# Mixture of experts on one Trainium2 core: four experts side by side in 32 slots each, their weights in 8 KB runs

## The chip, the core and the metric

The program runs on one core of a Trainium2 chip. The metric is the device time of one execution in microseconds (us), the median of several runs; lower is better. Engines are named as in the profile: PE is TensorE's matmuls and PEld its weight loads (LDWEIGHTS), DVE is VectorE, ACT ScalarE, POOL GpSimd, SP the engine that here only issues transfers (DMAs). MB is 10^6 bytes, KB 1024 bytes; "a piece" below is one 1024 KB load, 1.0486 MB.

## The reference, cut to what matters

Two transformer blocks run over 256 tokens of width 1024. The first has three attention branches; the second has a mixer, a cross attention and, last, a mixture of 32 experts. The change is in the last part, of which this is the core:

```python
xf = rmsnorm(h) * g                                  # 256 tokens x 1024
g_sel = argmax(softmax(xf @ w_group + b_group))      # one of 4 groups
top_p, top_i = top_k(softmax(logits of the 8 experts of the group), 2)
gate = p_g * top_p / sum(top_p)
...
for each expert e, for the tokens that took it:
    hid = silu(x @ w_gate[e]) * (x @ w_up[e])        # 1024 -> 512
    out = hid @ w_down[e]                            # 512 -> 1024
y[token] += gate * out;   h = h + y                  # float32 throughout
```

An expert has three float32 matrices of 2 MiB each: 6 MiB an expert, 201.3 MB for all 32. Each token takes two experts, so there are 512 assignments, 16 an expert on the average. Worked out with the reference's own router on the inputs that it draws by default, the fullest expert has 29 tokens.

## The kernel before, in words

**Up to about 600 us** the kernel works through the products with weights of both blocks (class `Stream`, line 213 issues their matmuls). Loads of weights run ahead on SP's queue, into a ring of 23 buffers of 8 KB per partition (`SLOTS = 23`, tag `s8`); the n-th piece goes into the buffer of piece n - 23 and its DMA waits until the last matmul that reads that piece is done. The experts' weights follow in the same stream and the same ring, so their first 23 pieces are fetched while the earlier products still run.

**The router** (lines 1640 to 1730) gives `rank[token, expert]`, the place of a token among those of its expert (0 where it isn't taken), and `gate`.

**The experts** are worked two at a time, in 16 pairs. An expert has `E_CAP = 64` slots; the two experts of a pair share the 128 slots, that is TensorE's 128 columns, one in columns 0 to 63 and the other in 64 to 127 (`HALVES`). For a pair:

- `select` (line 1768, on POOL except for the first pair) makes `sel[token, slot]`, the row's scale where the token has the slot, and `selg`, the gate there. It takes four TENSOR_SCALARs of 128x64 for each.
- `gather` (line 1783) is a matmul of `h` with `sel`; it gives the slots' inputs transposed, a 128x128 block for each of the 8 blocks of K, and line 1785 multiplies in the gain `gffn`.
- `up_and_gate` (line 1825): for each of the 8 blocks of K and for both experts a matmul of 64 columns by 512, for `w_gate` and then for `w_up`: 32 matmuls in the program, 64 instructions in the profile, since a float32 matmul is two instructions there. Lines 1831 to 1836 make the hidden values; `hid_T` (line 1845) transposes them.
- `down` (line 1854): 16 such matmuls, 32 instructions, over the two halves of the output's columns. `combine` (line 1865) gives the slots' outputs back to the tokens with `selg` transposed (line 1808), four matmuls of 128x512, and sums over the pairs in PSUM.

A pair has 12 pieces: two halves of each matrix for both experts. Each is loaded as `(k p) f -> p k f`: partition p gets rows p, 128 + p, 256 + p and 384 + p of the half, 2 KB of each (of `w_down`, half the columns of 512 rows, again 2 KB). The last six pieces are loaded in quarters of 1 KB runs, so that the last pair can begin on half the columns. The next pair's loads are issued as buffers come free; nothing else is on SP's queue until the output. PE's program order is fixed: up and gate of a pair, the gather of the next pair's inputs, `hid_T`, `down`, `combine`. The last pair does its four quarters of the output's columns one after the other (lines 1900 to 1925).

If an expert has more tokens than slots, a loop at the end (from line 1931) goes over all 32 experts again, loading their weights once more; with at most 29 tokens it isn't entered, before or after.

Of the kernel before, what the change touches and what calls it, by code (L numbers as in the profile page):

```python
# [15 lines left out]
OP = mybir.AluOpType  # L16
# [4 lines left out]
NT = 2          # token tiles  # L21
# [79 lines left out]
class Stream:  # L101
    """The products with weights, in one order: loads run ahead as far as there is room, the weights' split
    into two float32r parts two units ahead, and pump() issues the next units of products."""

    def __init__(self, k, parts):
        """parts: pairs of a job and a piece of its K"""
# [20 lines left out]
    def fetch(self):  # L127
# [53 lines left out]
    def idle(self):  # L181
        """no unit can be issued"""
# [5 lines left out]
    def pump(self, n=1):  # L188
        for _ in range(n):
# [11 lines left out]
            # low x high, high x high and high x low parts, the low parts of the weights last as they come last  # L201
# [31 lines left out]
class Kit:  # L233
# [42 lines left out]
    def take(self, shape, dt=F32):  # L276
        """one of the 8 KB pieces"""
# [4 lines left out]
    def rotations(self, *counts):  # L282
        """functions that hand out the 2 KB parts of one piece, counts[i] of them, in turn"""
# [15 lines left out]
    def carver(self):  # L299
        """a function that cuts tiles out of one piece"""  # L300
# [15 lines left out]
    def give(self, n):  # L316
        """n pieces have seen their last use"""
# [4 lines left out]
def block_kernel(ctx: ExitStack, tc: tile.TileContext, a: dict, out: bass.AP):  # L322
# [6 lines left out]
    # ================================================================ the products with weights, in order  # L329
# [53 lines left out]
    for e0 in range(0, 32, 2):  # L383
        pa_, pb_ = expert_srcs(e0), expert_srcs(e0 + 1)
# [40 lines left out]
    ACT.activation(sm(1), mhalf, AF.Sin)    # has the tables of the sine, which the copies need too, loaded early  # L425
# [6 lines left out]
    # later[p, k] = 1 where k > p  # L432
# [52 lines left out]
    def row_ss(src, c, ss, at=None, junk=None):  # L485
        """sums of squares of part c (a half) of the rows of src [P, NT, D], into ss [P, NT, parts]"""
# [5 lines left out]
    def row_scale(ss, name):  # L492
        """1 / rms of rows of D elements"""
# [13 lines left out]
    def split_evac(src, dstH, dstL, scale):  # L507
        """dstH + dstL = scale * src, dstH the rounded part"""
# [24 lines left out]
    def rope(x_, table, dst=None):  # L533
        """dst, x_ [P, NT, heads, 2 * half]; table: cosines and signed sines [P, NT, 2 * half], gains included"""
# [11 lines left out]
    def head_ss(src, heads, d):  # L546
        """sums of squares of the heads; src [P, heads, d]"""
# [9 lines left out]
    def out_of(dst, src, scale, on_dve):  # L557
        """dst = scale * src, from PSUM"""
# [25 lines left out]
    def pipeline(units, stages, fill):  # L584
        """stage s of unit i is issued in step i + s, products with weights after each step"""
# [16 lines left out]
    def exps(sc, rs, cols_, sums):  # L602
        """exp(rs * sc - max) of sc [P, n, nk]; column cols_[i] of rs and of sums belongs to sc[:, i]"""
# [13 lines left out]
    def weights_T(e):  # L617
        """transposes [P keys, n * blocks, P queries] of e [P, n, nk]"""
# [51 lines left out]
    def silu2(dsts, srcs, half):  # L670
        """dst = silu(2 * half * src) / half, for each token tile"""
# [6 lines left out]
    # ================================================================ first block  # L678
    # ---- x, transposed; its rows' scale comes in after the products
# [11 lines left out]
    # ---- rotary tables  # L691
# [7 lines left out]
    cs = cut([P, NT, 3, 16])       # cosines, sines, their opposites  # L699
# [22 lines left out]
    # cosines and signed sines of both halves, with the gains  # L722
# [16 lines left out]
    # masks: bf16 zeros and ones, times BIG on the tensor engine  # L739
# [10 lines left out]
    # ---- latent parts of branch B  # L750
# [15 lines left out]
    # evac of products that become heads: natural, one tile per token tile  # L766
# [1231 lines left out]
```

## Time and profile before

| | us |
|---|---|
| median of 3 runs (1085.7 to 1088.31) | 1085.85 |
| span of the profiled execution, first to last instruction | 1084.3 |
| start of the first pair's up and gate | 600.4 |
| start to start of one pair and the next | 29.96 |
| PE busy in the span | 1050.6 |

The median is 1.55 us above the profiled span; all sums below are made on the span and those 1.55 us are added at the end. The span falls into two parts: to 600 us the products of both blocks, with the experts' first loads under their last 80 us, and from there the 16 pairs. PE's busy time covers 97% of the span, but a busy PE may be one matmul after another or two side by side; which, is told by the time from one to the next.

### The profile page before, as it was taken

The page shows a single profiled execution, that of the slowest core. Times are in us where ns is not written, and L with a number is a line of the kernel's source. Part 1 is how long each engine was busy: PE and PEld are TensorE (multiplying, and loading weights), DVE is VectorE, ACT ScalarE, POOL GpSimd, SP SyncE. Part 2 cuts the span into 40 slices and gives each one's busy share as a digit, 9 for nine tenths or more (in the row PEclk, how much of TensorE's full clock was granted, in tenths as well). Part 3 has the DMA queues.
Part 4 walks back from the last instruction along what each step waited for, and adds up shares of the span by engine and source line. Part 5 has one row for each costly group of instructions (what it writes and reads, how often), then busy time and mean ns, then how long its engine had stood idle before and what let it go on. Part 6 is the DMA issues. An engine that isn't in the chain of part 4 may idle for free.

```text
span 1084.3 us, 13738 instructions
## 1 busy us (share of the span) xinstructions
PE 1050.6 (97%) x5377; PEld 690.3 (64%) x5377; DVE 463.1 (43%) x830; ACT 351.3 (32%) x669; POOL 178.9 (16%) x275
## 2 busy tenths in 40 slices
PE   8999999999999999999999999999999999999997
PEld 8978877788788877868878443444444444334444
DVE  5689675667666576767644311111111111101113
ACT  6656564454544653555543000000000000000000
POOL 4444001021131022200010211111111110111100
PEclk9999999999999999999999999999999999999999
DMA  6942434354564533635699899999999999999995
GB/s 214 385 141 83 154 117 155 117 194 146 167 169 155 192 118 115 231 119 187 237 308 331 317 387 386 386 387 386 386 387 386 386 386 386 387 386 386 386 372 176
DMA packets 153857, 289.91 MB, mean 267 GB/s; under 512 B 5841, under 2 KB 22078, under 8 KB 153790
## 3 DMA queue, kind: packets, MB, share of 16 engines
q1 hardware_dynamic: 152862, 286.46, 74.6%
q0 software_dynamic: 928, 2.54, 0.9%
q8 instruction: 44, 0.72, 0.3%
q14 instruction: 23, 0.19, 0.0%
HBM read 287.94 MB, written 1.05 MB: 267 GB/s over the span
## 4 chain that ended last, share of the span: by engine, by line
PE 88%; DVE 7%; ACT 2%; DMA 1%; issue 1%; SPq 0%; POOL 0%; ACTq 0%; POOLq 0%; DVEq 0%
PE pg L213 35%; PE psc L1825 20%; PE psc L1854 10%; PE pg L1865 5%; PE ptp L1783 3%; PE po L1783 3%; DVE s L165 2%; PE po L657 2%; DVE wk L1785 1%; PE ptp L1845 1%; PE psc L526 1%; PE psc L1165 1%; PE ptp L623 1%; PE psc L1521 1%; DVE s L560 1%
## 5 line engine op out<-in xcount | busy, mean ns | idle before, releaser
L213 PE MATMUL pg<-s,s 128*128 128x512 f32 (+5 forms) x2076 | 454.2, 376 | 4.2 <-ACT s L164 1.9
L213 PEld LDWEIGHTS pg<-s,s 128*128 128x128 f32 x2076 | 365.7, 189 | 71.3 <-ACT s L164 2.7
L1825 PE MATMUL psc<-s,wk 128*64 128x512 f32 (+1 forms) x1024 | 220.2, 587 | 0.0
L165 DVE TENSOR_TENSOR s<-s,s 128x1024 fp32r<-128x1024 f32 (+4 forms) x170 | 197.2, 1191 | 49.4 <-ACT s L164 49.2
L164 ACT ACTIVATE s<-s 128x1024 fp32r<-128x1024 f32 (+4 forms) x170 | 160.9, 995 | 13.3 <-DVE s L165 7.5
L1825 PEld LDWEIGHTS psc<-s,wk 128*64 128x64 f32 x1024 | 72.0, 137 | 136.2 <-issue 131.3
L1854 PE MATMUL psc<-s,wk 128*64 128x512 f32 (+1 forms) x544 | 113.9, 570 | 0.3 <-DMA s<-in_w_e_down_dram 0.3
L1832 DVE SCALAR_TENSOR_TENSOR wk<-wk,psc 128x512 f32<-128x512 f32 x16 | 11.0, 688 | 165.7 <-ACT wk L1831 165.7
L1854 PEld LDWEIGHTS psc<-s,wk 128*64 128x64 f32 x544 | 37.9, 137 | 64.4 <-issue 59.4
L1768 POOL TENSOR_SCALAR masks<-slot,rank,tiny 128x64 f32<-128x64 f32 x60 | 33.6, 577 | 233.9 <-PE po L1783 222.4
L477 POOL TENSOR_TENSOR sm<-sm,tiny 128x8 f32<-128x8 f32 (+2 forms) x28 | 36.0, 1297 | 179.6 <-DVE sm L481 146.4
L1865 PE MATMUL pg<-wk,wr 128*128 128x512 f32 (+1 forms) x136 | 59.8, 581 | 0.0
L1846 ACT ACTIVATE wk<-ptp 128x512 f32<-128x512 f32 (+1 forms) x17 | 9.7, 572 | 145.2 <-PE ptp L1845 145.2
L611 ACT ACTIVATE s<-psc,sm,tiny 128x256 f32<-128x256 f32 (+1 forms) x64 | 32.9, 520 | 72.1 <-DVE sm L608 71.6
L1768 POOL TENSOR_SCALAR selg<-slot,rank,el 128x64 f32<-128x64 f32 x60 | 33.6, 577 | 129.6 <-PE ptp L1808 129.6
L1858 DVE COPY wk<-psc 128x512 f32<-128x512 f32 (+1 forms) x18 | 11.7, 648 | 101.1 <-PE psc L1854 101.1
L1836 DVE TENSOR_TENSOR wk<-wk,psc 128x512 f32<-128x512 f32 (+1 forms) x16 | 10.7, 671 | 86.2 <-PE psc L1825 86.2
L1865 PEld LDWEIGHTS pg<-wk,wr 128*128 128x128 f32 x136 | 24.4, 189 | 35.1 <-issue 34.9
L1831 ACT ACTIVATE wk<-psc 128x512 f32<-128x512 f32 x16 | 9.6, 597 | 107.2 <-PE psc L1825 107.2
L1809 ACT ACTIVATE wr<-ptp 128x256 f32<-128x256 f32 x16 | 6.1, 383 | 107.3 <-PE ptp L1808 107.3
L1783 PEld LDWEIGHTS ptp<-masks,h 128*128 128x128 f32 x256 | 29.9, 191 | 14.1 <-issue 12.2
L1783 PE MATMUL ptp<-masks,h 128*128 128x128 f32 x256 | 33.2, 282 | 1.6 <-DVE masks L1768 1.0
(325 smaller groups left out, 885.8 us busy)
## 6 DMA issues: line engine op xcount, KB each, us to landing
s<-in_w_e_gate_dram SPq DMA_DIRECT2D x64, 1024.0 KB
s<-in_w_e_up_dram SPq DMA_DIRECT2D x62, 1024.0 KB
s<-in_w_e_down_dram SPq DMA_DIRECT2D x60, 1024.0 KB
s<-in_w_in_dram SPq DMA_DIRECT2D x36, 1024.0 KB
s<-in_w_ckv_dram SPq DMA_DIRECT2D x8, 1024.0 KB
s<-in_w_branch_dram SPq DMA_DIRECT2D x6, 1024.0 KB
s<-in_w_mem_kv_dram SPq DMA_DIRECT2D x4, 1024.0 KB
s<-in_w_out_dram SPq DMA_DIRECT2D x4, 1024.0 KB
```

Of the source, the lines that this page charges most:

```text
L164: self.k.nc.scalar.activation(hl[:, 0], w, AF.Copy)
L165: self.k.nc.vector.tensor_tensor(out=hl[:, 1], in0=w, in1=hl[:, 0].bitcast(F32), op=OP.subtract)
L213: mm(j.outs[t], lhsT=x_, rhs=hl[:, int(c == 2), i, :], start=step == ends[t][0], stop=step == ends[t][1])
L477: POOL.tensor_tensor(out=dst, in0=src, in1=e_.to_broadcast(shape), op=OP.pow)
L611: ACT.activation(e[:, i, :], sc[:, i, :], AF.Exp, bias=nb[:, i:i + 1], scale=rs[:, c:c + 1], accum_out=sums[:, c:c + 1])
L657: PE.matmul(o[:, hd % (out_heads or heads), :], lhsT=pt[:, i * nkt + kt, :], rhs=vals(kt, hd), start=(kt == 0), stop=(kt == nkt - 1))
L1768: eng.tensor_scalar(sel[:, t, 64 * i:64 * i + 64], slot, rank[:, t, e0 + i:e0 + i + 1], factor(t, e0 + i), op0=OP.is_equal, op1=OP.mult)
L1783: PE.matmul(tp[:, kb, :], lhsT=h[:, t, (k0 + kb) * P:(k0 + kb + 1) * P], rhs=sel[:, t], start=(t == 0), stop=(t == 1))
L1825: PE.matmul(p_[s0:s0 + sn, :], lhsT=xs[k0 // 4][:, kb, s0:s0 + sn], rhs=tiles(m, i, k0 // 4)[:, kb, cols], start=(k0 + kb == 0), stop=(k0 ...
L1854: PE.matmul(p_[s0:s0 + sn, :], lhsT=hT[:, kb, s0:s0 + sn], rhs=tiles(2, i, c)[:, kb, cols], start=(kb == 0), stop=(kb == 3))
L1858: DVE.tensor_copy(od, p_)
L1865: PE.matmul(outs[t][c], lhsT=sgT[:, t, :], rhs=od, start=start, stop=stop)
```

## The change

`E_CAP` is 32 and `QUAD` is 4: four experts at a time in 8 quads, each with 32 of the 128 columns, so 24 pieces a quad. `gate` and `up` of all quads but the first, and `down` of all quads but the last, are loaded as `(p k) f -> p (k f)`: partition p gets four neighbouring rows (two of `w_down`, whose piece is then 256 rows with all columns), 8 KB in one run. The order of the rows within K is thereby another one, so `gather_part` takes every fourth column of `h`, `hid_T` every second of `hid`, and a gain in the same order (`gpack`) is loaded. `select` makes all 128 slots with two TENSOR_TENSORs, now always on DVE. The last four pieces, not six, come in 1 KB runs.

```diff
-E_CAP = 64
+E_CAP = 32
+QUAD = 4
...
-        if i < n - 6:
+        if i < n - QUAD:
             dma(out=w, in_=src)
-        elif i % 2 == (n - 1) % 2:
+        elif i == n - 1:
             for c in range(2):
-                for x in (i - 1, i):
+                for x in range(n - QUAD, n):
                     cuts = [slice(0, 4)] if (c, x) != (1, n - 1) else [slice(0, 2), slice(2, 4)]
...
+    def packed_srcs(e):
+        r = []
+        for name in ("w_e_gate_2", "w_e_up_2", "w_e_down_2"):
+            src = a[name][0, e]
+            n, per = src.shape[0] // 2, src.shape[0] // 256
+            r.append([src[i * n:i * n + n, :].rearrange("(p k) f -> p (k f)", k=per) for i in range(2)])
+        return r
+
+    FIRST, LAST = 0, 32 // QUAD - 1
+
+    def packed(quad, m):
+        return quad != FIRST if m < 2 else quad != LAST
+
+    for quad in range(32 // QUAD):
+        both = [[f(QUAD * quad + i) for i in range(QUAD)] for f in (expert_srcs, packed_srcs)]
         for m in range(3):
-            for x_, y_ in zip(pa_[m], pb_[m]):
-                W.add_loads([x_, y_])
+            for half in range(2):
+                W.add_loads([both[packed(quad, m)][i][m][half] for i in range(QUAD)])
...
+    gpack = ct([P, 2, 4], "gpack")
+    POOL.dma_start(out=gpack, in_=a["norm_ffn_2"][0].rearrange("(j p k) -> p j k", j=2, k=4))
...
-    def select(e0, eng, factor):
-        sel = picks[factor is by_gate]
-        for t in range(NT):
-            for i in range(2):
-                eng.tensor_scalar(sel[:, t, 64 * i:64 * i + 64], slot, rank[:, t, e0 + i:e0 + i + 1],
-                                  factor(t, e0 + i), op0=OP.is_equal, op1=OP.mult)
+    def select(quad, factor):
+        sel = picks[factor is not by_row]
+        e0, n = QUAD * quad, P // QUAD
+        s4 = sel.rearrange("p t (e s) -> p t e s", e=QUAD)
+        shape = [P, NT, QUAD, n]
+        DVE.tensor_tensor(out=s4, in0=slot[:, None, None, 0:n].to_broadcast(shape),
+                          in1=rank[:, :, e0:e0 + QUAD, None].to_broadcast(shape), op=OP.is_equal)
+        f = r_f[:, :, None, None] if factor is by_row else factor[:, :, e0:e0 + QUAD, None]
+        DVE.tensor_tensor(out=s4, in0=s4, in1=f.to_broadcast(shape), op=OP.mult)
         return sel
...
-        for kb in range(n):
+        for kb in range(k0, k0 + n):
             for t in range(NT):
...
+                src = h[:, t, kb * P:(kb + 1) * P]
+                if pack:
+                    src = h[:, t, kb // 4 * 512:kb // 4 * 512 + 512].rearrange("p (q k) -> p k q", k=4)[:, kb % 4, :]
+                PE.matmul(tp[:, kb - k0, :], lhsT=src, rhs=sel[:, t], start=(t == 0), stop=(t == 1))
+        g = gpack.rearrange("p j k -> p (j k)") if pack else gffn
...
-                        for i, (s0, sn) in enumerate(halves):
+                        for i, (s0, sn) in enumerate(parts):
                             PE.matmul(p_[s0:s0 + sn, :], lhsT=xs[k0 // 4][:, kb, s0:s0 + sn],
-                                      rhs=tiles(m, i, k0 // 4)[:, kb, cols], start=(k0 + kb == 0), stop=(k0 + kb == 7))
+                                      rhs=rows(m, i, k0 + kb, cols), start=(k0 + kb == 0), stop=(k0 + kb == 7))
...
-    HALVES = [(0, 64), (64, 64)]
+    PARTS = [(E_CAP * i, E_CAP) for i in range(QUAD)]
...
+        def rows_of(m, i, kb, cols):
+            per = 4 if m < 2 else 2
+            if packed(quad, m):
+                w = W.weights(base + 2 * QUAD * m + QUAD * (kb // per) + i)
+                return w.rearrange("p (k f) -> p k f", k=per)[:, kb % per, cols]
```

Three places show what moves. On SP's queue, the loads around the end of the first pair before, whose buffers `s8` are numbered in the order of the ring:

```order
L134 DMA s8_805_4745<-in_w_e_up_2_dram 128x4x512
L134 DMA s8_806_4747<-in_w_e_up_2_dram 128x4x512
L134 DMA s8_807_4749<-in_w_e_down_2_dram 128x4x512
L134 DMA s8_808_4751<-in_w_e_down_2_dram 128x4x512
L134 DMA s8_826_4805<-in_w_e_down_2_dram 128x4x512
L134 DMA s8_851_4902<-in_w_e_down_2_dram 128x4x512
L134 DMA s8_864_4961<-in_w_e_gate_2_dram 128x4x512
L134 DMA s8_865_4963<-in_w_e_gate_2_dram 128x4x512
```

and around the end of the first quad's `up` after:

```order
L135 DMA s8_864_4962<-in_w_e_up_2_dram 128x4x512
L135 DMA s8_865_4964<-in_w_e_up_2_dram 128x4x512
L135 DMA s8_868_4996<-in_w_e_up_2_dram 128x4x512
L135 DMA s8_875_5058<-in_w_e_up_2_dram 128x4x512
L135 DMA s8_902_5338<-in_w_e_down_2_dram 128x2048
L135 DMA s8_903_5340<-in_w_e_down_2_dram 128x2048
L135 DMA s8_904_5342<-in_w_e_down_2_dram 128x2048
L135 DMA s8_905_5344<-in_w_e_down_2_dram 128x2048
```

The pieces have the same size and go into the ring in the same way, but from the first quad's `down` on a piece is one run of 2048 floats a partition instead of four of 512.

On PE, from the end of `up` of the second pair to the beginning of its `down` before (`masks` is `sel`, `psc`, `ptp` and `po` are PSUM tiles):

```order
L1825 MATMUL psc_929_5432<-s8_904_5313,wk_859_4956 64x512
L1825 MATMUL psc_929_5432<-s8_905_5315,wk_859_4956 64x512
L1783 MATMUL ptp_938_5470<-masks_242,h_69 128x128 x8
L1845 MATMUL ptp_939_5480<-ident_95,wk_860_4957 128x128 x4
L1783 MATMUL po_940_5486<-masks_242,h_69 128x128 x8
L1854 MATMUL psc_941_5500<-s8_906_5317,wk_861_4958 64x512
L1854 MATMUL psc_941_5500<-s8_907_5319,wk_861_4958 64x512
```

and from the end of `up` of the first quad after:

```order
L1848 MATMUL psc_901_5304<-s8_864_4962,wk_859_4957 32x512
L1848 MATMUL psc_901_5304<-s8_865_4964,wk_859_4957 32x512
L1848 MATMUL psc_901_5304<-s8_868_4996,wk_859_4957 32x512
L1848 MATMUL psc_901_5304<-s8_875_5058,wk_859_4957 32x512
L1830 MATMUL ptp_925_5384<-ident_95,selg_5214 128x128 x2
L1805 MATMUL ptp_926_5390<-masks_242,h_69 128x128 x8
L1871 MATMUL ptp_927_5400<-ident_95,wk_860_4958 128x128 x4
L1805 MATMUL po_928_5406<-masks_242,h_69 128x128 x8
L1880 MATMUL psc_929_5418<-s8_902_5338,wk_861_4959 32x512
L1880 MATMUL psc_929_5418<-s8_903_5340,wk_861_4959 32x512
L1880 MATMUL psc_929_5418<-s8_904_5342,wk_861_4959 32x512
L1880 MATMUL psc_929_5418<-s8_905_5344,wk_861_4959 32x512
```

Per block of K there are now four matmuls of 32 columns from four buffers instead of two of 64 from two; gather, transposes and combine are as many for a quad as they were for a pair.

On DVE, the same stretch before, from the second pair's hidden values (lines 1832, 1836) on:

```order
L1832 SCALAR_TENSOR_TENSOR wk_860_4957<-wk_860_4957,psc_928_5413 128x512
L1836 TENSOR_TENSOR wk_860_4957<-wk_860_4957,psc_929_5432 128x512
L1785 TENSOR_TENSOR wk_858_4955<-ptp_938_5470,gcol_135 128x512
L1785 TENSOR_TENSOR wk_859_4956<-po_940_5486,gcol_135 128x512
L1858 COPY wk_861_4958<-psc_942_5510 128x512
```

and after, from the first quad's (lines 1855, 1859) on:

```order
L1855 SCALAR_TENSOR_TENSOR wk_860_4958<-wk_860_4958,psc_899_5263 128x512
L1859 TENSOR_TENSOR wk_860_4958<-wk_860_4958,psc_901_5304 128x512
L1789 TENSOR_TENSOR masks_242<-slot_4948,rank_5212 128x256
L1792 TENSOR_TENSOR masks_242<-masks_242,tiny_71 128x256
L1807 TENSOR_TENSOR wk_858_4956<-ptp_926_5390,tiny_71 128x512
L1807 TENSOR_TENSOR wk_859_4957<-po_928_5406,tiny_71 128x512
L1789 TENSOR_TENSOR selg_5214<-slot_4948,rank_5212 128x256
L1792 TENSOR_TENSOR selg_5214<-selg_5214,el_5191 128x256
L1885 COPY wk_861_4959<-psc_930_5436 128x512
```

The two selections now stand on DVE between the hidden values and the gain, where before POOL made them by itself; POOL's only new row is the small load of `gpack`, ahead of its `slot` iota.

## Rows read from the trace of the kernel before

**Rows 1.** Page: engine busy share of the span, and moved GB/s in 40 slices.

```profile
PE 1050.6 (97%) x5377; PEld 690.3 (64%) x5377; DVE 463.1 (43%) x830; ACT 351.3 (32%) x669; POOL 178.9 (16%) x275
...
GB/s 214 385 141 83 154 117 155 117 194 146 167 169 155 192 118 115 231 119 187 237 308 331 317 387 386 386 387 386 386 387 386 386 386 386 387 386 386 386 372 176
```

**Rows 2.** Busy time of each engine by stretch; stretch, its length, engines, PEclk, DMA share, GB/s.

```profile
core 0: us, PE busy (x) PEld busy (x) DVE busy (x) ACT busy (x) POOL busy (x), PEclk, DMA share, GB/s
...
601.00:605.00 4.00, 4.00 (x24) 1.69 (x18) 2.92 (x17) 0.46 (x2) 0.00 (x0) 1.00 0.09 31
605.00:1050.00 445.00, 432.62 (x2112) 186.47 (x2112) 52.18 (x76) 32.61 (x60) 67.19 (x120) 1.00 1.04 385
1050.00:1066.00 16.00, 16.00 (x104) 7.71 (x102) 1.11 (x2) 0.98 (x2) 0.00 (x0) 1.00 1.07 343
1066.00:1070.00 4.00, 3.27 (x30) 2.35 (x30) 2.91 (x5) 1.15 (x3) 0.00 (x0) 1.00 0.47 152
```

**Rows 3.** The chain that ended last, one pair of it: start, us, what.

```profile
632.65 13.88 PE psc L1825 x64
...
651.75 7.02 PE psc L1854 x32
658.76 3.63 PE pg L1865 x8
...
662.61 1.43 PE psc L1825 x5
```

**Rows 4.** SP's loads at line 134: duration of an issue, min/median/max ns.

```profile
L134 SPq DMA_DIRECT2D s<-in_w_e_gate_dram x64: 367/2534/4171, 520.3 to 1032.5; - x64
L134 SPq DMA_DIRECT2D s<-in_w_in_dram x48: 367/368/1434, 2.9 to 398.5; - x48
```

**Rows 5.** Timeline of SP around the first pair's start: start, us, what.

```profile
587.37 17.04 SPq L134 DMA_DIRECT2D s<-in_w_e_down_dram  x4
604.50 0.46 SPq L134 DMA_DIRECT2D s<-in_w_e_gate_dram  x1
```

**Rows 6.** DMA packets from 700 to 1000 us, runs of 2 KB.

```profile
DMA packets 58271, 115.91 MB, mean 386 GB/s; under 512 B 1765, under 2 KB 1765, under 8 KB 58256
```

**Rows 7.** DMA packets from 1050 to 1066 us, runs of 1 KB.

```profile
DMA packets 5439, 5.49 MB, mean 343 GB/s; under 512 B 174, under 2 KB 5361, under 8 KB 5437
```

**Rows 8.** DMA packets from 129.5 to 131 us, `mem` in runs of 4 KB.

```profile
DMA packets 167, 0.62 MB, mean 412 GB/s; under 512 B 16, under 2 KB 16, under 8 KB 167
```

**Rows 9.** DMA queues from 609.1 to 609.6 us: packets, MB, share of 16 engines.

```profile
q1 hardware_dynamic: 93, 0.19, 98.0%
q14 instruction: 1, 0.01, 3.9%
```

**Rows 10.** Timeline of DVE at the first and the second pair.

```profile
596.67 0.98 DVE L1768 TENSOR_SCALAR masks<-slot,rank,tiny 128x64 f32<-128x64 f32 x4
...
598.68 0.42 DVE L1785 TENSOR_TENSOR wk<-ptp,gcol 128x256 f32<-128x256 f32 x1 [1.03 <-PE ptp L1783]
...
646.61 0.69 DVE L1836 TENSOR_TENSOR wk<-wk,psc 128x512 f32<-128x512 f32 x1 [5.49 <-PE psc L1825]
```

**Rows 11.** Timeline of the last quarter of the output's columns, on PE, DVE and SP.

```profile
1075.15 1.95 PE L1854 MATMUL psc<-s,wk 128*64 128x256 f32 x16
...
1077.15 0.42 DVE L1858 COPY wk<-psc 128x256 f32<-128x256 f32 x1 [1.47 <-PE psc L1854]
...
1079.45 1.39 SPq L1916 DMA_DIRECT2D out_dram<-s  x2
```

**Rows 12.** Engines by stretch, as in rows 2, around a fall of PEclk.

```profile
150.00:157.00 7.00, 4.97 (x27) 3.79 (x25) 5.17 (x10) 5.24 (x10) 0.00 (x0) 1.00 0.67 224
157.00:161.00 4.00, 4.00 (x12) 2.70 (x12) 0.85 (x2) 1.30 (x5) 0.00 (x0) 0.57 0.28 108
```

More of the change, by code (lines that the diff above doesn't have):

```diff
@@ L1761, in block_kernel, with gather_part, gather @@
     x_now = [w_.rearrange("p (k s) -> p k s", s=P) for w_ in work[0:2]]
[L1763 to L1778 removed]
+    def select(quad, factor):
[7 more added lines that the diff above has]
+        DVE.tensor_tensor(out=s4, in0=s4, in1=f.to_broadcast(shape), op=OP.mult)
+        return sel
+    by_row = None
+    def gather_part(sel, xg, k0, n, tag, pack=False):
         tp = ps([P, n, P], tag)
[L1781 removed]
+        for kb in range(k0, k0 + n):
             for t in range(NT):
[L1783 to L1787 removed]
+                src = h[:, t, kb * P:(kb + 1) * P]
[3 more added lines that the diff above has]
+        g = gpack.rearrange("p j k -> p (j k)") if pack else gffn
+        DVE.tensor_tensor(out=xg, in0=tp, in1=g[:, k0:k0 + n, None].to_broadcast([P, n, P]), op=OP.mult)
+    def gather(sel, pack):
         for k0 in (0, 4):
             xg = x_now[k0 // 4]
[L1791 removed]
+            gather_part(sel, xg, k0, 4, "o" if k0 else "tp", pack)
             yield xg
@@ L1812, in block_kernel, with up_and_gate @@
     WHOLE, HALF = [slice(0, 512)], [slice(0, 256), slice(256, 512)]
-    def up_and_gate(xg, halves, tiles, cuts=WHOLE):
+    def up_and_gate(xg, parts, rows, cuts=WHOLE):
         xs = []
@@ L1837, in up_and_gate, with hid_T @@
         return hid
-    def hid_T(hid, cuts=WHOLE):
+    def hid_T(hid, cuts=WHOLE, pack=False):
         tph = ps([P, 4, P], "tp")
@@ L1844, in hid_T, with down @@
             for kb in range(b.start, b.stop):
-                PE.transpose(tph[:, kb, :], hid[:, kb * P:(kb + 1) * P], ident)
+                src = hid[:, kb * P:(kb + 1) * P]
+                if pack:
+                    src = hid[:, kb // 2 * 256:kb // 2 * 256 + 256].rearrange("p (q k) -> p k q", k=2)[:, kb % 2, :]
+                PE.transpose(tph[:, kb, :], src, ident)
             ACT.activation(hT[:, b, :], tph[:, b, :], AF.Copy, scale=0.5)
         return hT
-    def down(hT, halves, tiles, c, dst, cols=slice(0, 512)):
+    def down(hT, parts, rows, c, dst, cols=slice(0, 512)):
         p_ = ps([P, 512], "sc")[:, cols]
         for kb in range(4):
-            for i, (s0, sn) in enumerate(halves):
-                PE.matmul(p_[s0:s0 + sn, :], lhsT=hT[:, kb, s0:s0 + sn], rhs=tiles(2, i, c)[:, kb, cols],
+            for i, (s0, sn) in enumerate(parts):
+                PE.matmul(p_[s0:s0 + sn, :], lhsT=hT[:, kb, s0:s0 + sn],
+                          rhs=rows(2, i, kb, slice(c * 512 + cols.start, c * 512 + cols.stop)),
                           start=(kb == 0), stop=(kb == 3))
@@ L1865, in combine @@
             PE.matmul(outs[t][c], lhsT=sgT[:, t, :], rhs=od, start=start, stop=stop)
-    HALVES = [(0, 64), (64, 64)]
-    xg = gather_first(select(0, DVE, by_row))
+    PARTS = [(E_CAP * i, E_CAP) for i in range(QUAD)]
+    xg = gather_first(select(0, by_row))
     xg = chain([next(xg)], xg)
@@ L1871, in block_kernel @@
     gate, most_i = gates_of_tokens()
-    selg = select(0, DVE, by_gate)
-    for pair in range(16):
-        base, last = first_expert + 12 * pair, pair == 15
+    selg = select(0, gate)
+    for quad in range(LAST + 1):
+        base, last = first_expert + 6 * QUAD * quad, quad == LAST
         cuts = HALF if last else WHOLE
-        def tiles(m, i, j):
-            return W.weights(base + 4 * m + 2 * j + i)
-        hid = up_and_gate(xg, HALVES, tiles, cuts)
-        for i in range(8):
+        def rows_of(m, i, kb, cols):
[3 more added lines that the diff above has]
+                return w.rearrange("p (k f) -> p k f", k=per)[:, kb % per, cols]
+            half = kb // 4 if m < 2 else cols.start // 512
+            c0 = half * 512 if m == 2 else 0
+            return W.weights(base + 2 * QUAD * m + QUAD * half + i)[:, kb % 4, cols.start - c0:cols.stop - c0]
+        hid = up_and_gate(xg, PARTS, rows_of, cuts)
+        for i in range(4 * QUAD):
             W.drop(base + i)
         W.top_up()
-        if pair == 0:
+        if quad == 0:
             sgT = gates_T(selg)
         if not last:
-            slots = gather(select(2 * pair + 2, POOL, by_row))
+            slots = gather(select(quad + 1, by_row), packed(quad + 1, 0))
             xg = [next(slots)]
-        hT = hid_T(hid, cuts)
+        hT = hid_T(hid, cuts, packed(quad, 2))
         if not last:
             xg = iter(xg + [next(slots)])
-            selg = select(2 * pair + 2, POOL, by_gate)
-            ods = [down(hT, HALVES, tiles, c, work[2 + c]) for c in range(2)]
+            selg = select(quad + 1, gate)
+            ods = [down(hT, PARTS, rows_of, c, work[2 + c]) for c in range(2)]
             for c in range(2):
-                combine(ods[c], sgT, yp, c, pair == 0, pair == 14)
-            for i in range(8, 12):
+                combine(ods[c], sgT, yp, c, quad == 0, quad == LAST - 1)
+            for i in range(4 * QUAD, 6 * QUAD):
                 W.drop(base + i)
@@ L1922, in block_kernel @@
     for q in range(4):
-        ods.append(down(hT, HALVES, tiles, q // 2, work[q % 2], HALF[q % 2]))
+        ods.append(down(hT, PARTS, rows_of, q // 2, work[q % 2], HALF[q % 2]))
         if q:
@@ L1926, in block_kernel @@
     finish(3)
-    for i in range(8, 12):
+    for i in range(4 * QUAD, 6 * QUAD):
         W.drop(base + i)
@@ L1959, in block_kernel, with rows_of @@
                             DVE.tensor_scalar(dst[:, t, at], slot, sh[:, t:t + 1], f, op0=OP.is_equal, op1=OP.mult)
-                hid = up_and_gate(gather(sel), [(0, P)], lambda m, i, j: ws[m][j])
+                def rows_of(m, i, kb, cols):
+                    j = kb // 4 if m < 2 else cols.start // 512
+                    c0 = j * 512 if m == 2 else 0
+                    return ws[m][j][:, kb % 4, cols.start - c0:cols.stop - c0]
+                hid = up_and_gate(gather(sel, False), [(0, P)], rows_of)
                 sgT = gates_T(selg)
@@ L1964, in block_kernel @@
                 for c in range(2):
-                    combine(down(hT, [(0, P)], lambda m, i, j: ws[m][j], c, work[c]), sgT, more, c, True, True)
+                    combine(down(hT, [(0, P)], rows_of, c, work[c]), sgT, more, c, True, True)
                     for t in range(NT):
```

16 lines of the change are left out of this document (2 added, 14 removed).

## The prediction

> **What bounds the kernel now.** I read the page first: PE is busy for 97% of the span, and from the second half on the transfers run at a flat 386 GB/s [rows 1]. Either could be the limit, so the next view is the table of stretches. From 605 to 1050 us PE works 432.6 of 445 us while the DMA engines are at a share of 1.04, that is, full [rows 2]. Both limits are reached at once.
>
> What PE does there is read from the chain: a pair's up and gate take 13.88 us for 64 instructions, its `down` 7.02 us for 32, and from one pair to the next it is 662.61 - 632.65 = 29.96 us [rows 3]. A 64-column instruction thus comes every 13.88/64 = 217 ns, while a `combine` instruction, which is as long but has all 128 columns, comes every 3.63/8 = 454 ns: the two experts run side by side. No wait for weights stands in this chain: PE goes on at its own pace.
>
> The transfers couldn't have fed a faster one. At 386 GB/s [rows 6] a piece (1.0486 MB) takes 2.717 us and a pair's twelve 32.6 us, more than PE's 29.96. PE starts with 23 pieces in the ring and eats the lead up: SP's last issue before the pairs begins at 587.37 and the next only at 604.50 us [rows 5], the DMA share between 601 and 605 is 0.09 [rows 2] (the ring is full), and from then on an issue takes a median 2534 ns instead of 368 [rows 4] (SP stands before a full queue). From 605 us to the end 445 x 0.385 + 16 x 0.343 + 4 x 0.152 = 177.4 MB come [rows 2], the 169 pieces that are left. The last are in at about 1069 us, and 15 us of work follow. So a faster PE alone would gain nothing but the tail; the price of a piece decides.
>
> **The price of an 8 KB run.** No such weights are in the trace, but three run lengths are. With 16 engines a run takes 16 x 1024/343 = 47.8 ns at 1 KB [rows 7], 16 x 2048/386 = 84.9 at 2 KB [rows 6] and 16 x 4096/412 = 159.1 at 4 KB [rows 8]. Each further KB costs 37.1 ns on both steps, so about 10.7 ns of a run are fixed, and 8 KB come to 159.1 + 4 x 37.1 = 307.5 ns. One packet of 8 KB is in the trace, a block of instructions in the middle of the saturated stretch: 3.9% of 16 engines for 0.5 us, 312 ns [rows 9]. That is 420 to 426 GB/s; I take 423, a piece in 2.48 us. The lower end is the 4 KB row's 412 GB/s, 2.545 us, were long runs cut or slowed; the end at zero gain is 2.717. A run that is slower per byte than 2 KB is excluded: no length in the rows is slower than a shorter one.
>
> The Trainium skill (DMA: Bandwidth & Descriptors, Measured) gives 425 GB/s for one 16 MB load with the pair's other core idle; by that figure alone a piece takes 2.47 us, an estimate that ends 2 us earlier than mine.
>
> **What it saves.** Of the 169 pieces after 605 us, 161 are now in 8 KB runs: 161 x (2.717 - 2.48) = 38.2 us. The other eight are the last quad's `down`, four in 2 KB and four in 1 KB runs; 1 KB costs 1.0486/0.343 = 3.06 us a piece, and two pieces fewer have it: 0.7 us.
>
> **TensorE.** A quad has as many groups of columns per block of K as it has experts, so with four side by side its up and gate take the 13.88 us of a pair and `down` 7.02; gather, transposes and `combine` are as many as for a pair. The quad takes about 30 us of PE where its 24 pieces take 24 x 2.48 = 59.5 us. PE becomes the engine that waits. If only two of the four ran at a time, it would be 30 + 20.9 = 51 us, still under 59.5. The loads of `h` and `hid` for every fourth or second column are not in the trace; from nothing to a tripling of the 4 us of gather they lie under the same cover, 27 us a quad. If that cover were gone (PE over 59.5 us a quad), each further us would count eight times.
>
> **The ring.** It holds less than a quad now (23 of 24), so I looked for a load that waits for PE. The tightest are a quad's first `down` pieces (16 to 19), freed at the end of `down`. The last piece of the quad lands 59.5 us after its start, and two thirds of `down` with PE at half clock follow: 70 us. The loads into these buffers are pieces 15 to 18 of the next quad, due at 59.5 + 15 x 2.48 = 97 us. 27 us to spare. At the beginning the first four buffers come free after the first half of gate, a quarter of 13.88 us after the start, as the first two did before.
>
> **Selections.** POOL's go (idle engine, nothing gained). On DVE two TENSOR_TENSORs of 128x256, at 0.42 us each by the nearest two-input row, take the place of four of 0.98 us in all [rows 10]. The first gather then needs both: before, it began after half of them. I count +0.2 us there (0 to 0.4). Later PE waits before each gather for hidden values and selection, 0.69 + 0.84 = 1.5 us [rows 10] that were none before; in a quad with 28 us to spare that costs nothing, and the last quad has no gather. `gpack`'s load stands on POOL's queue ahead of five short operations that are needed 30 us later: nothing.
>
> **The tail.** Now the last weights land about 1069 us and the end is at 1084.3: 15 us, because PE comes to the last four quarters late and does them in a row. With PE waiting, only the last quarter is left when its weights land: from its first matmul at 1075.15 [rows 11] to the end is 9.15 us, and about 1 us for the landing to be seen. After 7 us in which PE waited for 2, the granted clock was 0.57 over the next 4 us, that is, at its lower level of 1.2 GHz for most of them [rows 12]. PE will wait often now, so I expect that level at times; if it holds at the end, the quarter's 1.95 us and `combine`'s 1.1 double. 10.2 to 13.2 us instead of about 14.7; I take -3.0 us (-4.5 to -1.5).
>
> **Sum.** -38.2 - 0.7 + 0.2 - 3.0 = -41.7 us; span 1084.3 - 41.7 = 1042.6 us, and with 1.55 us around it 1044 us.
>
> **Rivals.**
> *A, the run length gives part of it:* long runs move at 412 GB/s as in [rows 8], 161 x 0.172 = 27.7 us; 1055 us. For it: 4 KB is the longest run of data that the trace shows. Against it: the even step of 37.1 ns per KB.
> *B, the run length gives nothing:* something beyond the runs holds 386 GB/s, or long runs are cut to 2 KB. Then only the tail and the 1 KB pieces gain: 1084.3 - 3.5 + 1.55 = 1082 us. Against it: [rows 8].
> *C, PE's clock falls and PE becomes the bound.* At 1.2 GHz PE's 29 us of matmuls a quad double: with waits about 61.5 us, over the 59.5 of the transfers. Seven quads in 430 us from 600.4, then the last one, whose 32 us from its start to the end (1052 to 1084 now) become some 58: span 1089, 1090 us, slower. It decides from 59.5 us a quad. Against it: a PE that is behind has no waits, and where it has none the clock stands at 1.00 [rows 2]; so it would catch up, and the case needs a low clock under full load. The skill (TensorE: Matmul & The Clock Gate, HAM oscillation) tells of a kernel whose matmuls between waits for weights ran at the lower clock each time, which speaks against this change; by that rule all of PE's quad is at 1.2 GHz and C is the result, and the trace agrees as far as [rows 12] go.
> *D, column groups of 32 don't run side by side.* Then an instruction comes every 454 ns instead of 108: 192 x 0.454 + 9 = 96 us a quad, eight of them 770 us, and the end is near 1382 us. Slower from (1084.3 - 10 - 600.4)/8 = 59.2 us a quad, which is (59.2 - 9 - 1.5)/192 = 254 ns an instruction. Against it: two groups of 64 do [rows 3].
> More than 32 tokens at an expert would be far worse (all weights once more, over 520 us), but the fullest has 29.
>
> **How the numbers follow.** The forecast has 0.73, A 0.13, B 0.06, C 0.04, D 0.04. About 0.3% (3 us) is what a measurement tells from no change. B ends at -0.35%, half of it within the bound: faster 0.73 + 0.13 + 0.03 + 0.01 (C in part) = 0.90, same 0.04, slower 0.06. The range takes the forecast with its bounds (426 GB/s and the short tail: 1040; a little more for what hides in the start) and A with the long tail (1057): 1036 to 1060. B, C and D, 0.14, are left out.
>
> **What would show it.** Right: about 423 GB/s flat from 605 to about 1007 us; quads 59.5 us apart; PE busy some 60% there, its waits ended by DMA; a 32-column instruction every 108 ns within a group of pieces (or 217 at the lower clock); the end about 12 us after the last weights. Wrong: 386 or 412 GB/s (B, A); DMA share under 1 with SP waiting for PE (C, D); PEclk near 0.5 while PE has no waits (C).

## The result, and the profile after

| | before | after |
|---|---|---|
| median (us) | 1087.08 | 1045.23 |
| lowest to highest of 4 runs (us) | 1085.7 to 1089.01 | 1044.64 to 1049.82 |
| profiled span (us) | 1084.3 | 1042.9 |
| first matmul of the experts (us) | 600.43 | 600.23 |
| from there to the end (us) | 483.9 | 442.7 |

The ratio is 0.962, 95% interval 0.959 to 0.965: 3.8% faster. Forecast were 1044 us and a span of 1042.6. The last row is worth having: the first 600 us are the same computation in every kernel here, but the experts' first matmul comes at 599.7 to 604.0 us in the ten profiles of this study. Time counted from that matmul leaves this spread out.

The page after, PE's line and the rate in 40 slices; they answer [rows 1]:

```profile
PE 930.0 (89%) x5073; PEld 622.4 (60%) x5073; DVE 445.5 (43%) x814; ACT 333.8 (32%) x637; POOL 112.5 (11%) x156
...
GB/s 221 385 127 120 112 152 145 117 163 166 157 228 108 231 120 94 165 219 105 200 279 293 354 332 418 420 421 418 420 419 419 421 419 420 419 419 420 420 407 241
```

Where 386 GB/s stood before, 418 to 421 stand now. The stretches (columns as in [rows 2]) and the packets from 700 to 1000 us, which answer [rows 6]:

```profile
605.00:1005.00 400.00, 316.35 (x1758) 122.90 (x1754) 35.79 (x65) 16.20 (x30) 0.00 (x0) 0.91 1.01 419
1005.00:1030.00 25.00, 17.33 (x162) 7.57 (x158) 4.60 (x9) 1.15 (x3) 0.00 (x0) 0.80 1.05 373
1030.00:1042.90 12.90, 6.68 (x68) 3.65 (x59) 3.40 (x8) 0.00 (x0) 0.00 (x0) 0.93 0.39 126
```

```profile
DMA packets 17275, 125.88 MB, mean 420 GB/s; under 512 B 1920, under 2 KB 1920, under 8 KB 1920
```

The DMA engines are still full (1.01); they now move more in the same time. PE is no longer full. The chain that ended last, a quad in the middle of it and then the end (start, us, what):

```profile
710.11 19.88 DMA s<-in_w_e_down_dram
...
730.06 19.88 DMA s<-in_w_e_gate_dram
...
750.00 19.89 DMA s<-in_w_e_up_dram
...
769.95 19.89 DMA s<-in_w_e_down_dram
```

```profile
1024.89 8.05 DMA s<-in_w_e_down_dram
1032.94 0.04 issue
1032.98 1.92 PE psc L1880 x26
1034.90 0.64 PE pg L1892 x2
```

Before, the pairs in this chain were PE alone [rows 3]. Now the quads are transfers alone: eight pieces from 710.11 to 730.06, 19.95 us, so 2.494 us a piece and 59.85 us a quad (769.95 - 710.11 = 59.84). After the last weights at 1032.94 us 10.0 us remain.

What PE does in the first quad and in a later one, from its timeline (start, us, engine, line, shapes, count, idle time before and what ended it):

```profile
600.16 3.64 PE L1848 MATMUL psc<-s,wk 128*32 128x512 f32 x32
...
739.15 4.49 PE L1848 MATMUL psc<-s,wk 128*32 128x512 f32 x34
745.00 1.05 PE L1848 MATMUL psc<-s,wk 128*32 128x512 f32 x2 [1.35 <-DMA s<-in_w_e_gate_dram]
747.49 1.89 PE L1848 MATMUL psc<-s,wk 128*32 128x512 f32 x2 [1.45 <-DMA s<-in_w_e_gate_dram]
749.98 4.09 PE L1848 MATMUL psc<-s,wk 128*32 128x512 f32 x28 [0.60 <-DMA s<-in_w_e_gate_dram]
...
775.22 3.97 PE L1805 MATMUL ptp<-masks,h 128*128 128x128 f32 x16 [1.67 <-DVE masks L1792]
```

Four pieces are needed for one group of matmuls. They land 2.5 us apart, PE issues the first matmul of each expert as its piece comes, and the rest of the group runs when the fourth is there. The first quad has its weights in the ring and shows the bare pace: 3.64 us for its first group of 32 instructions.

### The profile page after: what moved, and what is told of

The parts are those of the page before. It is cut to its first block, busy times and chain, and to the rows that moved or that the text cites. A ratio compares the mean times of both kernels' runs of the same rounds, so it can differ in the third digit from the quotient of the medians.

```text
span 1042.9 us, 12833 instructions
## 1 busy us (share of the span) xinstructions
PE 930.0 (89%) x5073; PEld 622.4 (60%) x5073; DVE 445.5 (43%) x814; ACT 333.8 (32%) x637; POOL 112.5 (11%) x156
## 3 DMA queue, kind: packets, MB, share of 16 engines
HBM read 287.94 MB, written 1.05 MB: 277 GB/s over the span
## 4 chain that ended last, share of the span: by engine, by line
PE 51%; DMA 38%; DVE 6%; ACT 2%; SPq 1%; issue 1%; POOL 0%; ACTq 0%; POOLq 0%; DVEq 0%
PE pg L214 36%; DMA s<-in_w_e_up_dram 13%; DMA s<-in_w_e_down_dram 12%; DMA s<-in_w_e_gate_dram 11%; DVE s L166 2%; PE po L674 2%; PE psc L1848 2%; PE psc L543 1%; PE psc L1182 1%; PE ptp L640 1%; PE psc L1538 1%; SPq L143 1%; PE psc L1880 1%; DVE s L577 1%; PE psc L685 1%
## 5 line engine op out<-in xcount | busy, mean ns | idle before, releaser
L1848 PE MATMUL psc<-s,wk 128*32 128x512 f32 (+1 forms) x1024 | 180.0, 697 | 63.3 <-DMA s<-in_w_e_up_dram 38.9
L1848 PEld LDWEIGHTS psc<-s,wk 128*32 128x32 f32 x1024 | 41.3, 127 | 195.2 <-issue 76.0
L1880 PE MATMUL psc<-s,wk 128*32 128x512 f32 (+1 forms) x576 | 71.0, 571 | 10.8 <-DMA s<-in_w_e_down_dram 10.4
L1855 DVE SCALAR_TENSOR_TENSOR wk<-wk,psc 128x512 f32<-128x512 f32 x8 | 5.5, 687 | 135.3 <-ACT wk L1854 135.3
L1859 DVE TENSOR_TENSOR wk<-wk,psc 128x512 f32<-128x512 f32 (+1 forms) x8 | 5.2, 654 | 120.6 <-PE psc L1848 120.6
L1880 PEld LDWEIGHTS psc<-s,wk 128*32 128x32 f32 x576 | 20.1, 116 | 55.6 <-issue 32.4
L1854 ACT ACTIVATE wk<-psc 128x512 f32<-128x512 f32 x8 | 4.8, 597 | 109.6 <-PE psc L1848 109.6
L1885 DVE COPY wk<-psc 128x512 f32<-128x512 f32 (+1 forms) x10 | 6.1, 611 | 68.5 <-PE psc L1880 68.5
L624 DVE TENSOR_REDUCE sm<-psc 128x2 f32<-128x512 f32 (+1 forms) x26 | 17.9, 689 | 32.6 <-PE psc L685 23.6
L1892 PE MATMUL pg<-wk,wr 128*128 128x512 f32 (+1 forms) x72 | 30.2, 559 | 0.0
L1805 PE MATMUL po<-masks,h 128*128 128x128 f32 x120 | 28.2, 388 | 0.0
L1805 PEld LDWEIGHTS po<-masks,h 128*128 128x128 f32 x120 | 27.6, 320 | 0.0
```

Source lines behind the costliest of these rows:

```text
L624: DVE.tensor_reduce(out=mx, in_=sc, axis=AX.X, op=OP.max)
L1805: PE.matmul(tp[:, kb - k0, :], lhsT=src, rhs=sel[:, t], start=(t == 0), stop=(t == 1))
L1848: PE.matmul(p_[s0:s0 + sn, :], lhsT=xs[k0 // 4][:, kb, s0:s0 + sn], rhs=rows(m, i, k0 + kb, cols), start=(k0 + kb == 0), stop=(k0 + kb == 7))
L1880: PE.matmul(p_[s0:s0 + sn, :], lhsT=hT[:, kb, s0:s0 + sn], rhs=rows(2, i, kb, slice(c * 512 + cols.start, c * 512 + cols.stop)), start=(kb ...
L1892: PE.matmul(outs[t][c], lhsT=sgT[:, t, :], rhs=od, start=start, stop=stop)
```

## The experiments

My theory was that two limits, PE at 29.96 us a pair and the transfers at 2.717 us a piece, stood side by side before, that each half of the change lifts one of them, and that afterwards a piece's time decides alone.

Each diff below is against the kernel after, with `...` for lines left out; the second kernel has the first one's edit as well. Ratios are to the kernel before as measured beside each: medians of 1087.86 us for the first four kernels and 1089.5 us for the others.

### One half alone: long runs for pairs

```diff
-E_CAP = 32
-QUAD = 4
+E_CAP = 64
+QUAD = 2
...
+        eng = DVE if quad == 0 else POOL
+        for t in range(NT):
+            for i in range(QUAD):
+                f = r_f[:, t:t + 1] if factor is by_row else factor[:, t, e0 + i:e0 + i + 1]
+                eng.tensor_scalar(sel[:, t, n * i:n * i + n], slot[:, 0:n], rank[:, t, e0 + i:e0 + i + 1],
+                                  f, op0=OP.is_equal, op1=OP.mult)
```

> One part alone: 8 KB runs, but experts two at a time in 64 slots as before, the selections on POOL as before. My theory: both limits were reached before, so a cheaper piece alone gains nothing. TensorE still needs 29.96 us a pair and now also the loads of every fourth column of h, which took 3.97 instead of 2.05 us per half gather after the change: 33.8 us a pair against 12 x 2.494 = 29.9 us of transfers. So about 15 x 3.85 = 58 us over before: 1144 us (1130 to 1150), TensorE busy without waits. Rival 1, the length of the runs alone gives the gain (only the transfers limited before): 1046 us. Rival 2, the strided loads lie under matmuls and cost nothing: 1084 us.

Measured: 1148.57 us, 1.057 of before (1.055 to 1.059); span 1145.8. Slower, as expected, by 4.6 us more than the middle of my range. The chain that ended last, one pair, and the loads of `h` into PE between 620 and 1000 us (count, busy us, mean ns, idle):

```profile
705.24 13.88 PE psc L1848 x64
719.12 3.94 PE ptp L1805 x16
...
724.58 3.72 PE po L1805 x16
728.30 7.02 PE psc L1880 x32
735.31 3.63 PE pg L1892 x8
...
739.16 13.88 PE psc L1848 x64
```

```profile
L1805 PEld LDWEIGHTS po<-masks,h 128*128 128x128 f32 x192 | 45.7, 329 | 0.0
```

From pair to pair it is 739.16 - 705.24 = 33.92 us instead of 29.96; up, gate and `down` take what they took, the gather 3.94 and 3.72 us. Long runs with two experts at a time, as before, are a loss of 5.7%.

### The same without the strided reads

```diff
-                if pack:
-                    src = h[:, t, kb // 4 * 512:kb // 4 * 512 + 512].rearrange("p (q k) -> p k q", k=4)[:, kb % 4, :]
...
-                if pack:
-                    src = hid[:, kb // 2 * 256:kb // 2 * 256 + 256].rearrange("p (q k) -> p k q", k=2)[:, kb % 2, :]
```

> As the pairs with 8 KB runs, but h and hid are read in plain column order, so the rows of the weights and of the inputs no longer match: the experts' values are wrong, the work is as much. It takes the cost of the strided loads out. My theory: TensorE's 29.96 us a pair stand alone and the transfers (29.9) fit just under them: 1086 us as before (1078 to 1090). The difference to the pairs with strided loads is then their price, about 58 us in 15 pairs. Rival, the transfers alone were the limit before: 1046 us.

Measured: 1088.18 us, 1.000 of before (0.998 to 1.001). The chain, the same loads, and the packets from 700 to 1000 us:

```profile
722.00 13.88 PE psc L1846 x64
735.88 2.00 PE ptp L1803 x16
...
739.30 1.79 PE po L1803 x16
...
751.95 13.88 PE psc L1846 x64
```

```profile
L1803 PEld LDWEIGHTS po<-masks,h 128*128 128x128 f32 x202 | 23.6, 192 | 0.0
```

```profile
DMA packets 17246, 125.68 MB, mean 419 GB/s; under 512 B 1916, under 2 KB 1916, under 8 KB 1916
```

The transfers do run at 419 GB/s here, and nothing is gained: PE's 29.95 us a pair decide, as before. The rival that the transfers alone were the limit has fallen. The strided reads cost 33.92 - 29.95 = 3.97 us a pair, 59.6 us in 15 pairs; from the first matmul to the end the two traces take 544.6 and 484.7 us, 59.9 apart. With pairs that is all on the path.

### The other half alone: quads with 2 KB runs

```diff
     def packed(quad, m):
-        return quad != FIRST if m < 2 else quad != LAST
+        return False
```

> The other part alone: four experts side by side in 32 slots, all weights in 2 KB runs as before (and no strided loads). My theory: the transfers bound at 386 GB/s, 2.717 us a piece, 65.2 us a quad, TensorE waits; only the tail and two pieces fewer in 1 KB runs gain: 1080 us (1076 to 1084). Rival, TensorE was the only limit before and the transfers can go faster than 386 GB/s at 2 KB if their buffers come free sooner: 1045 to 1060 us.

Measured: 1081.92 us, 0.995 of before (0.993 to 0.996); 477.2 us from the first matmul to the end. The stretches and the packets from 700 to 1000 us:

```profile
605.00:1005.00 400.00, 295.92 (x1636) 94.43 (x1624) 37.09 (x77) 15.45 (x29) 0.00 (x0) 0.88 1.04 382
```

```profile
DMA packets 58305, 115.93 MB, mean 386 GB/s; under 512 B 1769, under 2 KB 1769, under 8 KB 58294
```

PE is idle for 104 us of this stretch and the transfers stay at 386 GB/s: buffers that come free sooner don't make 2 KB runs faster. The two halves give +5.7% and -0.5% alone (the first 0.0% without its strided reads) and -3.8% together; the gain is in neither.

### The length of the run: quads with 4 KB

```diff
-            r.append([src[i * n:i * n + n, :].rearrange("(p k) f -> p (k f)", k=per) for i in range(2)])
+            halves = [src[i * n:i * n + n, :] for i in range(2)]
+            r.append([x_.rearrange("(j p k) f -> p j (k f)", j=2, k=2) if per == 4 else
+                      x_.rearrange("(k p) f -> p k f", k=2) for x_ in halves])
...
-                    src = h[:, t, kb // 4 * 512:kb // 4 * 512 + 512].rearrange("p (q k) -> p k q", k=4)[:, kb % 4, :]
+                    src = h[:, t, kb // 2 * 256:kb // 2 * 256 + 256].rearrange("p (q k) -> p k q", k=2)[:, kb % 2, :]
...
```

> The change with runs of 4 KB instead of 8 (two neighbouring rows of gate and up, one whole row of w_down). By a fixed part of about 10.7 ns a run and 37.1 ns per KB a piece takes 2.545 us at 412 GB/s, against 2.494 us as measured with 8 KB: 161 x 0.051 = 8.2 us more than the changed kernel, 1053 us (1050 to 1056). Rival, the rate grows only with the whole 8 KB row of a partition in one run: 386 GB/s, 1080 us. Rival, 4 KB is as good as 8: 1045 us.

Measured: 1057.65 us (1054.31 to 1060.15), 0.973 of before (0.971 to 0.976); span of the profiled run 1052.6, and 452.9 us from the first matmul to the end, 10.2 more than with 8 KB. Packets from 700 to 1000 us, and the loads of `h`:

```profile
DMA packets 31800, 122.73 MB, mean 409 GB/s; under 512 B 1868, under 2 KB 1868, under 8 KB 31789
```

```profile
L1807 PEld LDWEIGHTS po<-masks,h 128*128 128x128 f32 x112 | 13.7, 196 | 0.0
```

409 GB/s are 2.564 us a piece; 161 x (2.564 - 2.494) = 11.3 us, about what the trace lost. The median lies 1.65 us above my range and 4.65 above its middle. The rate is 409 and not the 412 of [rows 8], which is a row of 1.5 us: 161 x (2.564 - 2.545) = 3.1 us of it. The rest is less than the 5.8 us by which this kernel's own runs differ. So the rate rises with the run nearly as the step per KB said, 386, 409, 420 GB/s at 2, 4 and 8 KB. The row of loads is a finding by the way: a load that takes every second column costs 196 ns, nearly what neighbouring columns cost (192); every fourth costs 329.

### How much of PE is left

Sixteen matmuls a quad that nothing reads, and 40 of them in a second kernel:

```diff
+        if not last:
+            for _ in range(16):
+                PE.matmul(ps([P, 512], "sc"), lhsT=ident, rhs=h[:, 0, 0:512], start=True, stop=True)
         hT = hid_T(hid, cuts, packed(quad, 2))
```

> The changed kernel with 16 matmuls of 128x512 that nothing reads in each of the first seven quads, behind the first half of the gather: 16 x 2 x 0.454 = 14.5 us of TensorE a quad. By the durations of its instructions TensorE's own work is 13.9 + 7.0 (up and gate, down) + 7.9 (strided gather) + 0.7 + 3.6 + 0.2 + 2.5 of waits for DVE = 36 us a quad of 59.8, so 50 us still lie under the transfers: 1045 us as the changed kernel (1043 to 1049). Rival, the busy share of the trace (46 of 60 us) is TensorE's real need: then 60.5 us a quad, just over the transfers, and 1050 to 1058 us with the lower clock on top.

> The changed kernel once more, as the mark for the three beside it: 1045 us (1044 to 1049), 0.962 of before.

Measured: 1047.88 us (1047.16 to 1048.11) with the 16 and 1048.17 us (1043.83 to 1050.72) for the changed kernel beside it; both are 0.962 of before (0.960 to 0.964 and 0.965). From the first matmul to the end the two traces take 443.1 and 442.3 us. The stretch with the 16, and in it the dummies alone (count, busy us, mean ns, idle):

```profile
605.00:1005.00 400.00, 362.97 (x1970) 159.69 (x1966) 37.77 (x74) 16.20 (x30) 0.00 (x0) 0.97 1.01 415
```

```profile
L1925 PE MATMUL psc<-h,ident 128*128 128x512 f32 x224 | 97.6, 593 | 0.0
```

> The same with 40 such matmuls, 36.3 us a quad. By my account TensorE then needs 36 + 36.3 = 72.3 us a quad and is the bound: 600.4 + 7 x 72.3 + 32 for the last quad and its tail + 1.6 = 1140 us (1128 to 1150), the granted clock at 1.00 since nothing waits. Rival, the busy 46 us are its need: 82 us a quad, 1208 us. Rival of the prediction (C), the lower clock stays under full load: well over 1200 us.

PE's chain in the kernel with 40, and the stretch:

```profile
674.46 13.99 PE psc L1848 x128
...
694.18 34.41 PE psc L1925 x80
...
743.63 13.99 PE psc L1848 x128
```

```profile
605.00:1005.00 400.00, 389.74 (x1811) 179.43 (x1800) 30.05 (x60) 11.86 (x22) 0.00 (x0) 0.98 0.86 354
```

With 16 PE is busy 363 of 400 us and nothing is lost. With 40 it is bound: 1125.0 us, 1.033 of before (1.030 to 1.035), the DMA share at 0.86, a quad 743.63 - 674.46 = 69.17 us. That is 15 us less than I expected, and 3 under my range. A dummy instruction came every 34.4/80 = 0.43 us and not every 0.454, and PE's own work is 69.17 - 34.4 = 34.8 us a quad where I had counted 36; so a quad is 3.1 us shorter than the 72.3 I gave, and the profiled run began its experts 2.8 us later than I took (603.19 for 600.4), which takes a part of that back. So a quad leaves PE 59.85 - 34.8 = 25 us, and the trace's busy share (316 of 400 us, 47 us a quad) is not what PE needs. With more matmuls the granted clock is higher as well, 0.97 and 0.98 against 0.91, and with the 16 the time is the same: in this stretch the lower clock of the changed kernel costs nothing.

### A shorter end

```diff
-        return quad != FIRST if m < 2 else quad != LAST
+        return quad != FIRST if m < 2 else True
...
-            for c in range(2):
+            for c0, cn in ((0, 512), (512, 256), (768, 256)):
                 for x in range(n - QUAD, n):
...
+    def half_of_K(kb0, q):
+        for kb in (kb0, kb0 + 1):
+            for i, (s0, sn) in enumerate(PARTS):
+                PE.matmul(pd[q][s0:s0 + sn, :], lhsT=hT[:, kb, s0:s0 + sn],
+                          rhs=rows_of(2, i, kb, slice(q * 256, q * 256 + 256)), start=(kb == 0), stop=(kb == 3))
+    for q in range(4):
+        half_of_K(0, q)
     for q in range(4):
-        ods.append(down(hT, PARTS, rows_of, q // 2, work[q % 2], HALF[q % 2]))
+        half_of_K(2, q)
...
```

> A version meant to beat the changed kernel: the last quad's w_down cut by K like the others, its first half in 8 KB runs, the second in 2 KB runs (first two quarters of the columns) and 1 KB runs (the other two); the first half of K is multiplied for all quarters while the rest comes. Pieces: 4 x 2.49 + 2 x 2.72 + 2 x 3.06 = 21.5 us instead of 23.1, and the last quarter has half the matmuls, 0.96 us less: -2.6 us, 1042.5 us or 0.9975 of the changed kernel beside it. Rival, the more and smaller transfers at the end (13 instead of 9, of 128 and 256 KB) eat it up: the same time.

Measured: 1044.58 us (1041.91 to 1046.0), 0.959 of before (0.956 to 0.961), where the changed kernel beside it took 1048.17. The runs of the two overlap in part, and so do the intervals of their ratios; from the first matmul to the end it is 439.6 us against 442.3 and 442.7, so 2.7 to 3.1 us less, near the 2.6 expected. The chain's end, here and in `after_again`, from the landing of the last quad's `up`:

```profile
1013.86 15.40 DMA s<-in_w_e_down_dram
1029.26 0.04 issue
1029.30 1.91 PE psc L1961 x26
1031.21 1.06 PE pg L1892 x4
1032.27 1.03 PE po L1961 x16
```

```profile
994.59 19.91 DMA s<-in_w_e_up_dram
1014.50 0.04 issue
1014.54 2.39 PE psc L1848 x25
```

29.0 us pass from `up` (1013.79) to the end (1042.8) instead of 31.8 (1014.50 to 1046.3). From 1029.30 us on the chain is PE and then DVE, so what lands after that is not on the path; the 15.40 us of `down` before it are. This kernel's median is the lowest of this study, 0.3% under the changed kernel beside it but only 0.65 us under that kernel's first measurement (1045.23). The medians alone don't show the gain; the traces, one of each kernel and two of the changed one, do.

## Why the prediction was right, step by step

- **Both limits at once: shown.** Lifting the price of a piece alone gave 1.000 of before, and 1.057 with the strided reads that it brings; making PE faster alone gave 0.995.
- **The price of a piece: right in kind, 0.6% too low.** Taken were 423 GB/s and 2.48 us, measured are 420 and 2.494: 161 x 0.223 = 35.9 us saved instead of 38.2. The step per KB was the right row: it gave 307.5 ns for 8 KB, and the median of the 8 KB packets after is 313. The packet of [rows 9] came nearer, with 312, but by luck. It is not the only one, as the prediction has it; the trace before has five such packets of instructions between 605 and 1050 us, and others took longer. The queue from 605 to 1050, from 907.5 to 908 and from 984.8 to 985.4 us (packets, MB, share of 16 engines):

```profile
q14 instruction: 5, 0.04, 0.0%
...
q14 instruction: 1, 0.01, 4.2%
...
q14 instruction: 1, 0.01, 4.8%
```

4.2% of 16 engines for 0.5 us are 336 ns, or 390 GB/s, and 4.8% for 0.6 us are 461 ns, or 284 GB/s: by these rows the change would have gained little or lost. The Trainium skill (DMA: Bandwidth & Descriptors, Measured) has 425 GB/s for a 16 MB load; the trace gives 420 at this run length, and 386 at 2 KB with the engines just as full, so here the run's length decided and not the size of the load, 1 MB in both.
- **The tail: mis-sized the other way.** Taken was -3.0 us, an end 11.7 us after the last weights; it is 10.0 (gain 4.7, just past the bound of -4.5). The 1.5 us for a clock at its lower level weren't needed:

```profile
1025.00:1030.00 5.00, 5.00 (x54) 2.46 (x48) 1.27 (x3) 0.38 (x1) 0.00 (x0) 0.76 1.08 345
1030.00:1035.00 5.00, 4.86 (x61) 2.38 (x53) 1.34 (x4) 0.00 (x0) 0.00 (x0) 1.00 0.66 215
```

PE was busy 5.00 us from 1025 to 1030, at a granted clock of 0.76, and 4.86 from 1030 to 1035, at 1.00, the 2.4 GHz level. The two misses, +2.3 and -1.7, nearly cancel; that the sum came within 0.3 us of the span is partly luck.
- **TensorE under the transfers: right.** 34.8 us a quad (with 40 dummies) against the prediction's 31.5 and whatever the strided gather adds, which came to some 4 us. The cover was 25 us, not the 27 to 28 that it named before the gather's extra. The strided gather, for which it gave "from nothing to a tripling", nearly doubled: 3.97 us for one half of it where the plain reads take 2.00.
- **PE busy some 60%: wrong as a sign, not as a cost.** The share was 79%. A matmul that is issued ahead of its group's last piece runs alone: two instructions are 1.05 us of busy time, where in a full group of four one comes every 109 ns. At the lower clock it is more, as in the stretches of the first two single matmuls above:

```profile
745.00:746.00 1.00, 1.00 (x2) 0.13 (x2) 0.00 (x0) 0.00 (x0) 0.00 (x0) 1.00 0.99 410
747.50:749.40 1.90, 1.88 (x2) 0.15 (x2) 0.00 (x0) 0.00 (x0) 0.00 (x0) 0.51 1.02 423
```

Between these two PE waited 1.45 us; the granted clock was 1.00 in the first and 0.51, its lower level of 1.2 GHz, in the second, and the two instructions took 1.89 us. The strided gather adds its part. The 16 dummies are busy for 97.6 us of the stretch and raise the busy time by only 46.6, at the same time of the kernel.
- **32-column groups, all four side by side: shown.** 3.64 us for 32 instructions, to the end of the last, is 114 ns each, and 13.99 us for 128 in the kernel with 40 dummies is 109 ns. Rival D needed 254.
- **The ring, POOL, the first selection: right.** SP did wait for PE to free a buffer, 17 us in all between 605 and 1005 us beside 322 us of waits for its own transfers, but the DMA share of 1.01 shows that the engines had work meanwhile. The wait before the first gather was 1.34 us instead of 1.00, inside the 0 to 0.4 us that the prediction gave. One reading was wrong without harm: the row at 587.37 us in [rows 5] holds four loads, of which three were issued by 590.75 us and the fourth only at 604.04, so the ring was full from 590.75 to 604.04 us.
- **The rivals.** A (412 GB/s for long runs) is what 4 KB give, 409. B (386 GB/s stays) is what 2 KB give, 1081.92 us where it said 1082. C would need a quad of PE over 59.5 us. The granted clock did fall, to 0.91 on the average: between the two levels, full and half, that puts 18% of the stretch at the lower one. The Trainium skill (TensorE: Matmul & The Clock Gate, HAM oscillation) tells of a kernel whose matmuls between waits for weights ran at the lower clock each time; here that holds only for a part of them. With PE made the bound, by 40 dummies a quad, the granted clock was 0.98, so the rival's premise, a low clock under full load, is refuted.

## What to carry to other kernels

Where two resources are both full, test each half of a change against the other limit before adding gains up: here the halves were worth +5.7% and -0.5%, and -3.8% together. Read what an engine needs from the spacing of its instructions where it doesn't wait, not from its busy share, and what a run of a given length costs from the steps between the lengths that the trace has in number. A single packet of that very length can mislead: here five of them lay between 312 and 461 ns.

## What the runs showed of the hardware

- **Run length and rate with full queues:** 343 GB/s at 1 KB [rows 7], 386 at 2 KB, 409 at 4 KB, 420 at 8 KB, for loads of 1 MB (0.5 MB for most of those with 1 KB runs). With 16 engines that is 47.8, 84.9, 160.2 and 312.1 ns a run: each further KB costs 37.1, 37.7 and 38.0 ns, nearly the even step of the prediction. With the length the number of packets and the order of the addresses in memory change too; the runs don't separate these.
- **Strided loads into PE:** a float32 128x128 load takes 192 ns from neighbouring columns, 196 from every second and 329 from every fourth. The Trainium skill (SBUF — State Buffer, Door 1: The DMA port swizzle) speaks of 16-byte lines that want at least two accesses each; every second float32 column has two in such a line and every fourth one, and the three durations agree. That the lines are the cause was not tried.
- **The start varies:** the experts' first matmul comes at 599.7 to 601.2 us in five profiles and at 603.1 to 604.0 in the five others, whatever the kernel. In the five late traces the granted clock is 0.97 or 0.98 over 400 to 500 or 500 to 600 us, in the five early ones 1.00 over both; what brings it down there was not tried. The spread is as large as some of the differences here, which is why they were read from that matmul on.
